# Loading Q and K in gathered halves of 64 partitions in a one-core Q·Kᵀ kernel

## The chip, the core and the metric

The kernel runs on one core of a Trainium2 chip. A core has a matrix engine (PE, with its weight loads shown as PEld), a vector engine (DVE), a scalar engine (ACT), a general engine (POOL, GpSimd), a queue engine (SP), and 16 DMA engines that move data between HBM and the on-chip memory SBUF (128 partitions). Matrix results land in PSUM. The metric is the device time of one execution in microseconds (us); the median over several runs is compared. Beside it stands one profiled execution, from which all durations are taken.

## What is computed

For 8 batches of 12 heads, each with 1024 rows of 64 float32 values in Q and in K, the kernel computes all products of rows of Q with rows of K:

```python
q: (8, 12, 1024, 64) float32        k: (8, 12, 1024, 64) float32
return np.einsum('bhid,bhjd->bhij', q, k).astype(np.float32)   # (8, 12, 1024, 1024)
```

The inputs are 50.3 MB, the output 402.7 MB. The 96 heads are written as 4 MB each.

## The kernel before

**Blocks and heads.** The 96 heads are worked in nine blocks of 2, 2, 4, 8, 16, 16, 16, 16 and 16 heads (`sizes`). While the heads of one block are computed, Q and K of the next are loaded, cast to float16 and transposed. Q and K of a block stand in turn in one of two pairs of tiles (`qk_sb`), so that PE can read one block while the next is built.

**One head** (`scores`, L265 on). PE computes a head in four steps of two row tiles: each step has two weight loads (L436) and four matmuls (L439) into one half of PSUM. ACT copies each step's 128x2048 result into an output buffer (L297). When all four copies are done, SP issues the 4 MB store (L310). There are three output buffers (`o_sb`); ACT's first copy of a head waits until the store that last used its buffer has landed.

**Inputs of a block of 16 heads.** Q is loaded by one 4 MB DMA into the single input tile `x_sb` (32 KB in each of 128 partitions, L171); K later goes into the same tile, so its load waits until Q's casts have read the tile. POOL casts to float16 into one of three `half` tiles (L220): a chunk takes four casts of 32 partitions each, and a block has eight chunks, named (x, part, c): x is Q or K, `part` says which partitions it reads (0: 0 to 31 and 64 to 95; 1: 32 to 63 and 96 to 127), c is the half of the row. DVE transposes each chunk into `qk_sb` in 32x32 squares (L239). PE's first matmul of a block waits for all its transposes (`self.ready`).

**Order.** The order on each queue is the order in which the Python code records the instructions. `side` holds what is recorded after a given step of a given head: the transposes of the next block at the heads listed in `TURNS`, and the loads at the places in `LOADS`, which for blocks 4 and on is `{1: 1, 7: 1}`: behind step 1 of heads 1 and 7. Both loads are issued from ACT's queue, so the DMA instruction stands behind that step's copy. `to_half` records casts as soon as a chunk's load has been recorded and a `half` tile is due to come free. An `Engine` counts its finished instructions in a semaphore; `settle` makes an engine wait for its own.

**The last head** (`scores_split`, L316 on) is stored in two parts. Its first part goes out by a DMA of POOL (L374) that scatters rows by a list of indices, `place`, eight of which lie out of bounds; those rows are stored by four small DMAs.

```python
at = LOADS.get(i, {1: 1, 7: 1})
if n in at:
    side[at[n]] = side.get(at[n], []) + [lambda: next_load(act)]
```

Of the kernel before, what the change touches and what calls it, by code (L numbers as in the profile page):

```python
# [63 lines left out]
def kernel(  # L64
# [14 lines left out]
    of = out.rearrange("b h i j -> (b h) i j")  # L79

    sizes = [2, 2, 4, 8] + [16] * ((BH - 16) // 16)
    PE_BLOCKS, EARLY = 2, 3
    NMAX = max(sizes)
    CHUNK, HALVES = 64 * 32, 3
    TURNS = (3, 4, 5, 6, 10, 11, 12, 13)
    APART = (16, 48)
    LOADS = {0: {}, 1: {}, 2: {1: 3}, 3: {2: 1}}

    pool = ctx.enter_context(tc.tile_pool(name="sb", bufs=1))
    psum = ctx.enter_context(  # L90
# [8 lines left out]
    ]  # L99
    o_sb = [pool.tile([P, NT, S], F32, name=f"o_sb{i}", tag=f"out{i}") for i in range(3)]  # L100
    rest_q = pool.tile([P, 64], F16, name="rest_q", tag="rest_q")
    place_sb = pool.tile([P, 1], I32, name="place", tag="place")
    place_f = pool.tile([P, 1], F32, name="place_f", tag="place_f")
    ps_all = psum.tile([P, 4 * S], F32, tag="po")
# [35 lines left out]
    input_busy = []  # L140
    outs = Ring(o_sb)
    input_landing = [Landing(nc, f"x{i}_in") for i in range(2)]
    tail_landing = Landing(nc, "tail_out")
    rest_landing = Landing(nc, "rest_out")
    store_landing = {id(t): Landing(nc, f"out{i}_out") for i, t in enumerate(o_sb)}

    class Block:
        def __init__(self, i, first, N):
            self.i, self.first, self.N = i, first, N
            self.by_pe = i < PE_BLOCKS  # L150
            self.R = N * S // P
            self.elems = self.R * D
            self.cut = max(1, -(-self.R * 32 // CHUNK))
            self.raw = [None] * 2
            self.landed = [[] for _ in range(2)]
            self.rows = [None] * 2
            self.halves = {}
            self.qk = qk_sb[i % 2]
            self.ready = []
            self.over = []  # L160

        def load(self, x, eng, landing=None):
            events = []
            if self.raw[x] is None:
                at = x * self.elems if self.i == EARLY else 0
                self.raw[x] = x_sb[:, at : at + self.elems]
                landing = input_landing[x]
                events = list(input_busy)
            src = flat[x][self.first * S : (self.first + self.N) * S]
            eng.wait(events)  # L170
            dma = eng.eng.dma_start(  # L171
                out=self.raw[x], in_=src.rearrange("(p r) d -> p (r d)", p=P)
            )
            self.landed[x].append(landing.start(dma))

        def load_head(self, n, x, eng, landing):
            start = (self.first + n) * S
            m = S * D // P
            dma = eng.eng.dma_start(
                out=self.raw[x][:, n * m : (n + 1) * m],  # L180
                in_=flat[x][start : start + S].rearrange("(p r) d -> p (r d)", p=P),
            )
            self.landed[x].append(landing.start(dma))

        def cast_rows(self, x):
            n = S * D // P
            buf, events, busy = rooms.next()
            rows = buf[:, : 2 * n].rearrange("p (r h d) -> p r h d", h=2, d=D)
            for h in range(2):
                done = gps.run(  # L190
                    lambda: nc.gpsimd.tensor_copy(  # L191
                        out=rows[:, :, h],
                        in_=self.raw[x][:, h * n : (h + 1) * n].rearrange(
                            "p (r d) -> p r d", d=D
                        ),
                    ),
                    events + [self.landed[x][h]],
                )
            self.rows[x] = rows, done, busy
            return done  # L200
# [9 lines left out]
        def cast_quads(self, x, part, c):  # L210
            m = self.R // self.cut
            buf, events, busy = (rooms if self.i == PE_BLOCKS else halves).next()
            dst = buf[:, : m * 32]
            raw = self.raw[x].rearrange("p (r h d) -> p r h d", h=2, d=32)
            for half in range(2):
                b = 2 * half + part
                for h in range(2):
                    q0 = 32 * (2 * half + h)
                    done = gps.run(
                        lambda: nc.gpsimd.tensor_copy(  # L220
                            out=dst[q0 : q0 + 32].rearrange("p (r d) -> p r d", d=32),
                            in_=raw[32 * b : 32 * b + 32, c * m : (c + 1) * m, h],
                        ),
                        events + self.landed[x],
                    )
            self.halves[x, part, c] = dst, done, busy
            if self.i >= EARLY:
                input_busy[:] = [done]
            return done
# [35 lines left out]
        def scores(self, n, side, regions, w):  # L265
            half, g = divmod(n, self.N // 2)
            cs = slice(half * D, (half + 1) * D)
            qT = self.qk[0].rearrange("c (g m t) -> c g t m", t=NT, m=P)
            kT = self.qk[1].rearrange("c (g j) -> c g j", j=S)
            buf, out_free, out_busy = outs.next()  # L270
            written = {}
            for u in range(NT // w):
                ps, ps_free, ps_busy = regions.next()
                for tt in range(w):
                    stationary = qT[cs, g, w * u + tt]
                    done = pe.run(
                        lambda: load_weights(stationary, half * D),
                        self.ready if n == 0 and u == 0 else [],
                        signal=False,
                    )  # L280
                    for j in range(2):
                        at = tt * S + j * 512
                        done = pe.run(
                            lambda: multiply(
                                ps[:, at : at + 512],
                                stationary,
                                kT[cs, g, j * 512 : (j + 1) * 512],
                                half * D,
                            ),
                            ps_free,  # L290
                            signal=tt == w - 1 and j == 1,
                        )
                dst = buf[:, w * u : w * u + w].rearrange("p t j -> p (t j)")
                by_dve = w == 1 and u % 2
                copier = dve if by_dve else act
                copied = copier.run(
                    lambda: (nc.vector.tensor_copy if by_dve else nc.scalar.copy)(  # L297
                        out=dst, in_=ps[:, : w * S]
                    ),
                    out_free + [done],  # L300
                )
                written[copier] = copied
                ps_busy.append(copied)
                for do in side.get(u, []):
                    do()
            self.over = [done]
            sp.wait(written.values())
            if self.first + n == 0:
                sp.wait(blocks[EARLY].landed[0])
            dma = nc.sync.dma_start(  # L310
                out=of[self.first + n].rearrange("(p t) j -> p (t j)", p=P),
                in_=buf.rearrange("p t j -> p (t j)"),
            )
            out_busy.append(store_landing[id(buf)].start(dma))
# [145 lines left out]
    for b in blocks[:EARLY]:  # L460
# [7 lines left out]
        else:  # L468
            for x in range(2):
                b.load(x, sp, Landing(nc, f"e{b.i}{x}"))  # L470
    stream = [(b, x) for b in blocks[EARLY:] for x in range(2)]

    casts = [
        (i, c) for i in range(PE_BLOCKS, len(blocks)) for c in blocks[i].chunks()
    ]

    def next_load(eng):
        if stream:
            b, x = stream.pop(0)
            earlier = (b.i, 0) if x else (b.i - 1, 1)  # L480
            assert b.i == EARLY or not any((i, c[0]) == earlier for i, c in casts)
            b.load(x, eng)

    for x in range(2):
        next_load(sp)
# [17 lines left out]
    def to_half(last):  # L503
        while casts:
            i, c = casts[0]
            if i > last or (blocks[i], c[0]) in stream:
                return
            if not (rooms if i == PE_BLOCKS else halves).free():
                return
# [9 lines left out]
    def block(i, heads, regions, w):  # L519
        b = blocks[i]  # L520
        nxt = blocks[i + 1] if i + 1 < len(blocks) else None
        for n in heads:
# [11 lines left out]
            elif nxt:  # L534
# [1 line left out]
                at = TURNS if i > EARLY else [m * b.N // len(parts) for m in range(len(parts))]  # L536
                some = [s for m, s in zip(at, parts) if m == n]
                side = {0: [lambda s=s: transposed(nxt, s) for s in some]}
            at = LOADS.get(i, {1: 1, 7: 1})
            if n in at:  # L540
                side[at[n]] = side.get(at[n], []) + [lambda: next_load(act)]
            if i == len(blocks) - 1 and n == b.N - 1:
# [5 lines left out]
    for b in blocks[:PE_BLOCKS]:  # L548
        for x in range(2):
            b.cast_rows(x)  # L550
    nc.gpsimd.wait_ge(gps.sem, gps.count)
    to_half(2)

    quarters = Ring([ps_all[:, i * S : (i + 1) * S] for i in range(4)])
# [6 lines left out]
    halves_ps = Ring([ps_all[:, 2 * S :], ps_all[:, : 2 * S]])  # L561
    halves_ps.busy = [quarters.busy[2] + quarters.busy[3], quarters.busy[0] + quarters.busy[1]]
    block(0, [1], halves_ps, 2)
    for i in range(1, len(blocks)):
        block(i, range(blocks[i].N), halves_ps, 2)
    sp.wait([(c, c.count) for c in [*store_landing.values(), tail_landing, rest_landing]])
# [30 lines left out]
```

## Time and profile before

| | |
|---|---|
| median of 3 runs | 1059.84 us (1059.79 to 1059.84) |
| the profiled execution's own time | 1060.67 us |
| its span, first to last instruction | 1058.9 us |
| PE, ACT, DVE, POOL busy | 66%, 66%, 41%, 34% of the span |
| moved between HBM and SBUF | 453.21 MB, mean 428 GB/s |
| chain that ended last | DMA 65%, ACT 15%, PE 8%, DVE 6%, POOL 4% |

All durations come from the profiled execution. In the profile a group of instructions is named by its line, engine, operation and tiles (written tile first); "idle before" is the time its engine stood still just before it, with what ended that. DMA queue q1 belongs to SP, q10 to ACT, q0 to POOL. The trace also holds a record of each DMA packet with queue, size, start and duration. It doesn't name the DMA engine, but packets of one engine follow each other so closely that they can be strung together by their ends and starts.

### The profile page before, as it was taken

How to read it: one execution, taken by the hardware profiler on the slowest of the kernel's cores; microseconds unless marked ns; L12 is line 12 of the kernel's file. 1: busy time of each engine (PE TensorE's matmuls, PEld its weight loads, DVE VectorE, ACT ScalarE, POOL GpSimd, SP SyncE). 2: the span in 40 equal slices, each digit the busy share in tenths (PEclk: the TensorE clock that was granted, in tenths of full speed). 3: DMA queues.
4: the chain of work that ended last, by engine and by line, in shares of the span. 5: the costliest groups of instructions: out<-in, count | busy, mean ns of one | idle time of the engine just before them, and what ended most of it. 6: DMA issues, size and time to landing. Idle time of an engine off the chain costs nothing.

```text
span 1058.9 us, 3350 instructions
## 1 busy us (share of the span) xinstructions
PE 702.3 (66%) x1572; PEld 127.4 (12%) x802; DVE 435.4 (41%) x57; ACT 695.6 (66%) x385; POOL 358.3 (34%) x223
## 2 busy tenths in 40 slices
PE   6875754857477747657765756775674777787771
PEld 1111100111011101101110111110110111111110
DVE  2995939029194008539002917600580930000001
ACT  4766755857477748567765856775674777777771
POOL 7926555056280019065005609100822900000000
DMA  9999999999999999999999999999999999999998
GB/s 378 434 424 433 435 431 434 420 423 428 434 431 433 436 417 435 432 433 433 435 418 436 436 427 430 433 436 429 430 428 428 436 434 434 432 429 433 434 431 366
DMA packets 17186, 453.21 MB, mean 428 GB/s; under 512 B 1929, under 2 KB 1929, under 8 KB 2953
## 3 DMA queue, kind: packets, MB, share of 16 engines
q1 hardware_dynamic: 15008, 408.03, 89.5%
q10 hardware_dynamic: 2016, 42.99, 9.8%
q0 software_dynamic: 144, 1.97, 0.4%
q8 instruction: 9, 0.15, 0.0%
q14 instruction: 9, 0.07, 0.0%
HBM read 50.33 MB, written 402.78 MB: 428 GB/s over the span
## 4 chain that ended last, share of the span: by engine, by line
DMA 65%; ACT 15%; PE 8%; DVE 6%; POOL 4%; issue 1%; SPq 0%; ACTq 0%
DMA out_dram<-o_sb 60%; ACT o_sb L297 15%; PE ps_all L439 7%; DVE kT L239 4%; POOL half L220 3%; DMA x_sb<-in_q_dram 2%; DMA x_sb<-in_k_dram 2%; DVE qT L239 1%; DMA o_sb<-in_q_dram 0%; DVE x_sb L345 0%; DVE o_sb L345 0%; PE ps_all L253 0%; POOL qT L191 0%; DVE kT L260 0%; ACT kT L260 0%
## 5 line engine op out<-in xcount | busy, mean ns | idle before, releaser
L439 PE MATMUL ps_all<-kT,qT 64*128 64x512 f16 x1536 | 696.4, 617 | 327.1 <-ACT o_sb L297 310.0
L297 ACT COPY o_sb<-ps_all 128x2048 f32<-128x2048 f32 (+1 forms) x380 | 687.7, 1859 | 331.6 <-DMA out_dram<-o_sb 286.3
L220 POOL CAST half<-x_sb 32x2048 f16<-32x2048 f32 x176 | 332.5, 1889 | 482.7 <-DMA x_sb<-in_q_dram 307.9
L239 DVE STREAM_TRANSPOSE qT<-half 128x2048 f16<-128x2048 f16 x22 | 202.5, 9477 | 274.0 <-POOL half L220 274.0
L239 DVE STREAM_TRANSPOSE kT<-half 128x2048 f16<-128x2048 f16 x22 | 202.4, 9536 | 132.6 <-POOL half L220 132.6
L436 PEld LDWEIGHTS <-qT 64*128 64x128 f16 x768 | 124.0, 162 | 896.3 <-issue 875.9
L345 DVE COPY x_sb<-ps_all 128x2048 f32<-128x2048 f32 x1 | 2.3, 2292 | 174.0 <-PE ps_all L439 174.0
L374 POOL DMA_INDIRECT out_dram<-x_sb,place x1 | 1.2, 1157 | 176.6 <-DVE x_sb L345 176.6
L239 DVE STREAM_TRANSPOSE kT<-kT 128x1024 f16<-128x1024 f16 x2 | 9.3, 4856 | 0.0
L239 DVE STREAM_TRANSPOSE qT<-qT 128x1024 f16<-128x1024 f16 x2 | 9.2, 4782 | 0.0
L220 POOL CAST qT<-o_sb 32x1024 f16<-32x1024 f32 x8 | 8.3, 1036 | 1.1 <-DMA o_sb<-in_q_dram 0.7
L220 POOL CAST kT<-o_sb 32x1024 f16<-32x1024 f32 x8 | 8.3, 1036 | 0.5
L260 DVE COPY qT<-ps_all 128x1024 f16<-128x1024 f16 x2 | 2.4, 1224 | 11.4 <-PE ps_all L253 11.4
L253 PE MATMUL ps_all<-ident,qT 128*128 128x128 f16 x16 | 2.1, 311 | 7.1 <-POOL qT L191 7.0
L297 DVE COPY o_sb<-ps_all 128x1024 f32<-128x1024 f32 x4 | 4.9, 1225 | 4.4 <-PE ps_all L439 4.4
L345 ACT COPY x_sb<-ps_all 128x2048 f32<-128x2048 f32 (+1 forms) x2 | 3.7, 1860 | 2.1 <-PE ps_all L439 2.1
L260 ACT COPY kT<-ps_all 128x1024 f16<-128x1024 f16 x1 | 1.0, 1013 | 5.1 <-PE ps_all L253 5.1
L366 POOL COPY rest_q<-qT 64x8 f16<-64x8 f16 x4 | 0.6, 197 | 9.9 <-DVE kT L239 9.9
L345 DVE COPY o_sb<-ps_all 128x2048 f32<-128x2048 f32 x1 | 2.3, 2292 | 3.7 <-PE ps_all L439 3.7
L191 POOL CAST qT<-o_sb 128x512 f16<-128x512 f32 x4 | 2.3, 614 | 4.0 <-DMA o_sb<-in_q_dram 4.0
L260 ACT ACT_TABLE_LOAD x1 | 1.3, 1283 | 2.8 <-issue 2.8
L260 DVE COPY kT<-ps_all 128x1024 f16<-128x1024 f16 x1 | 1.2, 1225 | 4.4 <-PE ps_all L253 4.4
(18 smaller groups left out, 14.5 us busy)
## 6 DMA issues: line engine op xcount, KB each, us to landing
out_dram<-o_sb SPq DMA_DIRECT2D x95, 4096.0 KB, 21.8
x_sb<-in_q_dram ACTq DMA_DIRECT2D x5, 4096.0 KB, 25.2
x_sb<-in_k_dram ACTq DMA_DIRECT2D x5, 4096.0 KB, 23.4
x_sb<-in_q_dram SPq DMA_DIRECT2D x1, 2048.0 KB, 14.5
x_sb<-in_k_dram SPq DMA_DIRECT2D x1, 2048.0 KB, 18.9
out_dram<-o_sb SPq DMA_DIRECT2D x1, 2048.0 KB, 17.4
o_sb<-in_k_dram ACTq DMA_DIRECT2D x4, 256.0 KB, 5.2
o_sb<-in_q_dram SPq DMA_DIRECT2D x4, 256.0 KB, 5.4
```

Of the source, the lines that this page charges most:

```text
L191: lambda: nc.gpsimd.tensor_copy(out=rows[:, :, h], in_=self.raw[x][:, h * n : (h + 1) * n].rearrange("p (r d) -> p r d", d=D),),
L220: lambda: nc.gpsimd.tensor_copy(out=dst[q0 : q0 + 32].rearrange("p (r d) -> p r d", d=32), in_=raw[32 * b : 32 * b + 32, c * m : (c + 1) * ...
L239: lambda: nc.vector.transpose(out=dst, in_=buf.rearrange("p (r i) -> p r i", i=32)),
L253: lambda: nc.tensor.transpose(t_ps[:, t], rows[:, t], ident),
L260: lambda: copy(out=dst, in_=t_ps.rearrange("c t m -> c m t")), [done]
L297: lambda: (nc.vector.tensor_copy if by_dve else nc.scalar.copy)(out=dst, in_=ps[:, : w * S]),
L345: lambda: (nc.vector.tensor_copy if copier is dve else nc.scalar.copy)(out=dst[:, t * S : (t + w) * S], in_=ps[:parts, : w * S]),
L366: lambda: nc.gpsimd.tensor_copy(out=packed[:, t, 0, :, c], in_=rows[:, t, :, c]),
L374: nc.gpsimd.indirect_dma_start(out=out.rearrange("b h (m t) j -> (b h m) (t j)", t=T), out_offset=bass.IndirectOffsetOnAxis(ap=place_sb, a ...
L436: return nc.tensor.ldweights(stationary, tile_position=(at, to))
L439: return nc.tensor.add_instruction(mybir.InstMatmult(name=nc.get_next_instruction_name(), ins=[nc.tensor.lower_ap(moving), nc.tensor.lower ...
```

## The change

Blocks 0 to 4 are loaded as before. From block 5 on, the load of Q or of K becomes two gathers of POOL's DMA queue, each over all 128 partitions of `x_sb`, with a list of 128 row indices in which the indices of 64 partitions lie out of bounds. The gather for part 0 has valid rows in partitions 0 to 31 and 64 to 95, the one for part 1 in the others, which are the partitions that the casts of that part read. The lists, two columns for each of the four blocks, are written once by POOL (an iota and four memsets). Each cast now waits for its own part's load.

The loads of blocks 4 to 7 for the block after them stand at step 2 of heads 0, 4, 8 and 11, and the transposes at heads 2, 3, 6, 7, 10, 11, 13 and 14. In POOL's queue a gather stands behind all casts recorded before it. It waits for ACT to have finished the copies recorded so far (the third copy of that head) and for POOL's own instructions. ACT issues only block 4's two loads. The instructions of PE, SP and DVE, and their order, stay as they were.

```diff
-    TURNS = (3, 4, 5, 6, 10, 11, 12, 13)
+    TURNS = (2, 3, 6, 7, 10, 11, 13, 14)
     LOADS = {0: {}, 1: {}, 2: {1: 3}, 3: {2: 1}}
+    LATER = {0: 2, 4: 2, 8: 2, 11: 2}
...
+        def load_part(self, x, part):
+            self.raw[x] = x_sb[:, : self.elems]
+            c = 2 * (self.i - WHOLE - 1) + part
+            gps.count += 1
+            dma = nc.gpsimd.indirect_dma_start(
+                out=self.raw[x],
+                out_offset=None,
+                in_=flat[x].rearrange("(p r) d -> p (r d)", r=self.R),
+                in_offset=bass.IndirectOffsetOnAxis(ap=rows_sb[:, c : c + 1], axis=0),
+                bounds_check=BH * S // self.R - 1,
+                oob_is_err=False,
+                engine_sem=gps.sem,
+            )
+            self.landed[x][part].append(part_landing[part].start(dma))
+            gps.settle()
...
-                        events + self.landed[x],
+                        events + self.landed[x][part],
...
     def next_load(eng):
-        if stream:
-            b, x = stream.pop(0)
+        if not stream:
+            return
+        b, x, part = stream.pop(0)
+        pending = [(i, c[0], c[1]) for i, c in casts if i >= EARLY]
+        if b.i <= WHOLE:
             earlier = (b.i, 0) if x else (b.i - 1, 1)
-            assert b.i == EARLY or not any((i, c[0]) == earlier for i, c in casts)
+            assert b.i == EARLY or earlier not in [c[:2] for c in pending]
             b.load(x, eng)
+        else:
+            assert pending[:1] in ([], [(b.i, x, part)])
+            gps.wait([(act, act.count)])
+            gps.settle()
+            b.load_part(x, part)
...
-            at = LOADS.get(i, {1: 1, 7: 1})
+            at = LOADS.get(i, LATER)
...
     block(0, [1], halves_ps, 2)
+    gps.settle()
+    gps.run(
+        lambda: nc.gpsimd.iota(
+            rows_sb,
+            pattern=[[P, G], [0, 2]],
+            base=blocks[WHOLE + 1].first * S // blocks[WHOLE + 1].R,
+            channel_multiplier=1,
+        )
+    )
+    gps.settle()
+    by_part = rows_sb.rearrange("p (g h) -> p g h", h=2)
+    for p in range(0, P, 32):
+        gps.run(
+            lambda: nc.gpsimd.memset(by_part[p : p + 32, :, 1 - p // 32 % 2], 2 * BH * S)
+        )
+    gps.settle()
```

More of the change, by code (lines that the diff above doesn't have):

```diff
@@ L81 @@
     sizes = [2, 2, 4, 8] + [16] * ((BH - 16) // 16)
-    PE_BLOCKS, EARLY = 2, 3
+    PE_BLOCKS, EARLY, WHOLE = 2, 3, 4
     NMAX = max(sizes)
     CHUNK, HALVES = 64 * 32, 3
-    TURNS = (3, 4, 5, 6, 10, 11, 12, 13)
+    TURNS = (2, 3, 6, 7, 10, 11, 13, 14)
     APART = (16, 48)
     LOADS = {0: {}, 1: {}, 2: {1: 3}, 3: {2: 1}}
+    LATER = {0: 2, 4: 2, 8: 2, 11: 2}
     pool = ctx.enter_context(tc.tile_pool(name="sb", bufs=1))
@@ L101 @@
     rest_q = pool.tile([P, 64], F16, name="rest_q", tag="rest_q")
+    G = (BH - sum(sizes[: WHOLE + 1])) // NMAX
+    rows_sb = pool.tile([P, 2 * G], I32, name="rows", tag="rows")
     place_sb = pool.tile([P, 1], I32, name="place", tag="place")
@@ L142 @@
     input_landing = [Landing(nc, f"x{i}_in") for i in range(2)]
+    part_landing = [Landing(nc, f"part{i}_in") for i in range(2)]
     tail_landing = Landing(nc, "tail_out")
@@ L154, in __init__ @@
             self.raw = [None] * 2
-            self.landed = [[] for _ in range(2)]
+            self.landed = [[[], []] for _ in range(2)]
             self.rows = [None] * 2
@@ L173, in load @@
             )
-            self.landed[x].append(landing.start(dma))
+            event = landing.start(dma)
+            for part in self.landed[x]:
+                part.append(event)
+        def load_part(self, x, part):
[13 more added lines that the diff above has]
+            gps.settle()
         def load_head(self, n, x, eng, landing):
@@ L182, in load_head @@
             )
-            self.landed[x].append(landing.start(dma))
+            self.landed[x][0].append(landing.start(dma))
         def cast_rows(self, x):
@@ L196, in cast_rows @@
                     ),
-                    events + [self.landed[x][h]],
+                    events + [self.landed[x][0][h]],
                 )
@@ L308, in scores @@
             if self.first + n == 0:
-                sp.wait(blocks[EARLY].landed[0])
+                sp.wait(blocks[EARLY].landed[0][0])
             dma = nc.sync.dma_start(
@@ L470 @@
                 b.load(x, sp, Landing(nc, f"e{b.i}{x}"))
-    stream = [(b, x) for b in blocks[EARLY:] for x in range(2)]
+    stream = [
+        (b, x, part)
+        for b in blocks[EARLY:]
+        for x in range(2)
+        for part in range(1 if b.i <= WHOLE else 2)
+    ]
     casts = [
@@ L505, in to_half @@
             i, c = casts[0]
-            if i > last or (blocks[i], c[0]) in stream:
+            if i > last or (blocks[i], c[0], c[1] * (i > WHOLE)) in stream:
                 return
@@ L550 @@
             b.cast_rows(x)
-    nc.gpsimd.wait_ge(gps.sem, gps.count)
+    gps.settle()
     to_half(2)
@@ L563 @@
     block(0, [1], halves_ps, 2)
+    gps.settle()
[13 more added lines that the diff above has]
+        )
+    gps.settle()
     for i in range(1, len(blocks)):
```

## Prediction

> **What bounds the kernel now.** I read the page's DMA rows first, then the stages, the waits and the chain. The share of the 16 DMA engines by slices, and the queues:
>
> ```profile
> DMA  9999999999999999999999999999999999999998
> ...
> q1 hardware_dynamic: 15008, 408.03, 89.5%
> q10 hardware_dynamic: 2016, 42.99, 9.8%
> q0 software_dynamic: 144, 1.97, 0.4%
> ```
>
> q1 holds what SP issues (the stores), q10 what ACT issues (the loads), q0 what POOL issues. The shares sum to 99.7%: nearly every DMA engine carries a packet at nearly every moment. The stages (busy us of PE, PEld, DVE, ACT, POOL, then clock, DMA share, GB/s) say the same; no compute engine fills its stage:
>
> ```profile
> 60.00:200.00 140.00, 86.50 (x192) 15.31 (x95) 96.80 (x11) 86.64 (x49) 64.21 (x34) 1.00 1.00 430
> 376.00:552.00 176.00, 116.14 (x258) 20.74 (x128) 73.57 (x8) 116.34 (x64) 60.46 (x32) 1.00 1.00 431
> 830.00:1030.00 200.00, 149.78 (x332) 26.64 (x166) 27.47 (x4) 149.81 (x84) 16.40 (x24) 1.00 1.00 432
> ```
>
> The waits agree. ACT, the only engine that feeds stores, waits for output buffers, so engines that seem late here are being held by the DMA:
>
> ```profile
> ACT o_sb L297 <- DMA out_dram<-o_sb: 286.3, 84, 8.9
> ```
>
> In the trace's packet records a 32 KB packet takes 1.213 us, and packets of one engine start 1.209 us apart with no gap. A completion packet (4 bytes) adds 6 ns. So the time is the DMA work of an engine, plus about 2 us before the first stores can run and about 2 us in which engines end unevenly (the first at 1053.8, the last at 1057.3). Only three things can move it: DMA work, its evenness over the engines, or an engine that finds no packet.
>
> **What the change does to the DMA work.** The bytes stay: blocks 5 to 8 had 8 loads of 128 rows of 32 KB, now 16 gathers with 64 valid rows each, 1024 packets both times (64 per engine). The trace has one such transfer, the scatter of the last head, whose list has 8 indices out of bounds (its group, then its row among the DMA issues with the us from issue to landing):
>
> ```profile
> L374 POOL DMA_INDIRECT out_dram<-x_sb,place x1 | 1.2, 1157 | 176.6 <-DVE x_sb L345 176.6
> ```
>
> ```profile
> out_dram<-x_sb,place POOLq DMA_INDIRECT x1, 18.6
> ```
>
> Its 144 packets on q0 are 120 of 16384 bytes (0.611 us) and 24 of 4 bytes (9 ns): 16 completions and 8 rows out of bounds. An index out of bounds thus costs a 4-byte packet. The 8 stood on one engine, each behind one store packet (1.22 us apart). Their partitions are 16-19 and 48-51, so rows p and p+32 share an engine, and a gather of partitions 0-31 and 64-95 should leave 4 valid rows on each of the 16: no engine gets more than another.
> - Added short packets per engine: 16 x (4 out of bounds + 1 completion) - 8 x 1 = 72, x 6 ns = **+0.4 us** (+0.65 at their full 9 ns). Were rows cut into 16 KB packets, 64 x (2 x 0.611 - 1.213) = +0.6 more; I take no cut, as the scatter's rows were not cut.
> - Slow reads. In the stretches of these 8 loads, packets exceeded 1.213 us by 2.95 us (loads) and 0.95 us (stores beside them), meaned over 16 engines: 3.36 us of it in the four Q loads, at heads 1 to 3 of a block, and 0.54 in the four K loads at heads 7 to 9. Nothing shows whether Q's data or the place in the block is the reason. If Q, nothing changes; if the place, the second half of Q escapes (-1.7) and the four places may all be quiet (-2.8) or all as bad (+2.8). I take **-0.7**, between no change and half of Q's excess. Bounds: -3.9 (all gone) and +2.8.
>
> **What it moves on the other engines.** ACT loses 8 issues of 0.33 us: ACT idles 2.3 us a head for its buffer, so 0. POOL gains 16 x 1.16 = 18.6 us of issue, one iota and four memsets. The issues fall where POOL waits for a load or for ACT's signal, and the casts behind them are counted below. The five setup instructions stand before the casts of block 3's last chunk, where POOL waits 3.79 us for DVE (52.3 to 56.1); at the last head the same kinds take 0.13 (iota) and 0.15 us (memset), about 1.1 us with the settling between them, so 0. Were that cover gone, block 4's Q load, issued at 63.83 right behind these casts, and with it block 4's start, which has no cover left (below), would come up to 1.1 us later, with up to 1.1 us on the end. SP's queue and PE's order stay; DVE's transposes keep their order, and DVE does nothing else there.
>
> The added waits: POOL waits for ACT's third copy of heads 0, 4, 8, 11, then issues. Behind it in POOL's queue stand only the casts of that quarter, behind these the transposes, behind them PE at the next block. Whether the DMA runs out of packets there is decided by the last two quarters, which come close together. The rows for casts and transposes are these (start, us):
>
> ```profile
> 459.30 31.13 POOL L220 CAST half<-x_sb 32x2048 f16<-32x2048 f32 x16 [35.77 <-DMA x_sb<-in_k_dram]
> ...
> 467.06 36.80 DVE L239 STREAM_TRANSPOSE kT<-half 128x2048 f16<-128x2048 f16 x4 [30.06 <-POOL half L220]
> ```
>
> that is 7.8 us for the 4 casts of a chunk, 15.6 a quarter, and 9.2 us a transpose. A gather's landing is an estimate: first packet 5.0 us after issue (scatter: 1034.74 to 1039.8), up to 1.2 for the store packet in front, 4 data rows each with a store packet (2.42 each), 4 short ones and the completion behind one store packet each (1.21): 5.0 + 1.2 + 9.7 + 6.1 = 22.0 us. From the third issue: landed 22.0; cast 37.6; ACT's signal for the fourth comes at 3 heads x 9.76 + 4.9 of load work = 34.2, so POOL is later and issues at 37.6; landed 59.6; first chunk cast 67.4; two transposes 85.8; PE's first four matmuls (1.9) 87.7. ACT's buffer for the next block is free 8 x 9.76 + 2 x 4.9 - 5.7 = 82.2 after the third issue. **The block starts 5.5 us late.** What that costs, block 4 shows today:
>
> ```profile
> 169.21 18.23 DVE kT L239 x2
> 187.44 0.05 issue
> 187.49 1.94 PE ps_all L439 x4
> ...
> 189.44 1.88 ACT o_sb L297
> ```
>
> The buffer's last store packet was done at 180.5, so ACT was 9.0 us late, and the store queue just covered it: the busy engines fell from 16 to 14 for one moment at 197.75. The cover is two stores of 9.7 us in the queue, less ACT's 7.5 and the issue. So 5.5 costs nothing; it costs from 9 us (fastest engines) to 11 us (the slowest, which sets the end).
>
> **Sum.** On the profiled execution: span 1058.9 + 0.4 - 0.7 = 1058.6. That execution took 1060.67 us, 0.83 over the median of the runs; I carry the difference over: 1059.84 - 0.3 = **1059.5 us**.
>
> [...]
>
> **Rivals.**
> - *Slower: the fourth quarter lands too late.* Place: the start of blocks 5 to 8. It decides when ACT is over 9 to 11 us late; two landings stand in series, so 2 to 3 us more per landing suffice. At 25.2 us (a whole load's median landing today) ACT is 11.9 late, which costs 0.9 to 2.9 at four starts: +4 to +12, say 1067.5. One reason would be a gather's issue held by a transpose that runs beside it: the third is issued 4.3 us before DVE is done with the second quarter, the fourth 1.4 or 10.6 us before the end of one or both transposes of the third, so 11.2 to 20.4 us late, +1 to +46, about 1083 in the middle. [...] Against: casts, which use SBUF too, take 1886 to 1895 ns whether a transpose runs beside them or not. Chance 0.23, of it 0.05 for the held issue.
> - *Faster: the slow reads go.* All 3.9 us gone, 0.4 added: 1056.3. For it: K's loads have almost none, so reads beside stores need not be slow. Against: half the loads still stand near the places that are slow now. Chance 0.20 for more than 2.1 us.
> - *It doesn't do what it says.* Rows out of bounds move data after all: 16 x 64 packets more, 64 x 1.21 = +77 us, 1137. Against it the 4-byte packets. Chance 0.01; 0.01 for gather rows that move slower than the scatter's.
> - *As forecast*, within 0.2% (2.1 us; about what a measurement of this kernel can tell from no change): 0.55.
>
> Range: 1056.3 (slow reads gone) to 1068 (late by a slower landing); outside lie about 0.1 above and 0.05 below. Faster 0.20, same 0.55, slower 0.25.
>
> **What would show it.** Right: q0 holds 16 x 144 + 144 = 2448 packets with 33.55 + 1.97 MB, DMA share 1.00 in every stage, ACT's wait for PE at block starts about 5 us and no slice below 410 GB/s after the first. Wrong: landings over 25 us, ACT's waits for PE over 9 us at blocks 5 to 8 and a DMA share under 1.00 just after them; or a higher q0 share than 64 x 1.213 us an engine gives (7.3% of the span, with the scatter 7.8%), which would mean slower reads.

## The result, and the profile after

The changed kernel takes **1067.62 us** (median of 6 runs, 1066.58 to 1073.12) against 1059.80 us for the kernel before in the same series (6 runs, 1059.56 to 1059.84): ratio 1.0083, 95% interval 1.0061 to 1.0105, **7.8 us slower**. The forecast was 1059.5; its range reached 1068.0. The profiled execution of the changed kernel took 1066.58 us, the fastest of its six runs, with a span of 1064.3 us; against the profiled execution before that is 5.91 us more.

The page of the changed kernel, the same rows as before: busy tenths and GB/s of the DMA in 40 slices, then the queues with packets, MB and share, then the HBM counter.

```profile
DMA  9999999999999999999999999999999999999997
GB/s 374 433 434 433 434 432 433 431 433 410 432 432 433 432 430 425 432 433 429 433 415 432 421 432 432 430 433 417 427 425 426 433 427 426 432 433 431 432 433 334
...
q1 hardware_dynamic: 15008, 408.03, 89.3%
q0 software_dynamic: 2448, 35.53, 8.2%
q10 hardware_dynamic: 864, 9.44, 2.1%
...
HBM read 83.89 MB, written 402.78 MB: 457 GB/s over the span
```

The packets on q0 are the 2448 that were forecast, with 33.55 + 1.97 MB: each index out of bounds cost a 4-byte packet here (9 ns) and moved nothing (453.21 MB before and after). Their share is 8.2% of the span, where the prediction named more than 7.8% as its sign of slower reads. (The HBM counter shows 83.89 MB read, before 50.33: it counted the 16 x 64 rows of 32 KB, 33.55 MB, that were never moved.) The shares still sum to 99.6%, but of a longer span: q0 and q10 now take 10.3% of 1064.3 us, before 10.2% of 1058.9. The stages (PE, PEld, DVE, ACT, POOL, clock, DMA share, GB/s) look almost as before:

```profile
60.00:200.00 140.00, 87.15 (x193) 15.36 (x95) 96.45 (x11) 87.27 (x49) 64.85 (x35) 1.00 1.00 431
376.00:552.00 176.00, 116.25 (x257) 20.74 (x128) 73.87 (x8) 116.42 (x65) 64.37 (x36) 1.00 1.01 430
830.00:1030.00 200.00, 145.29 (x322) 25.92 (x160) 36.88 (x4) 145.49 (x81) 31.60 (x32) 1.00 1.00 431
```

A full DMA share with 1 GB/s less: the engines carried a packet all the time but for 0.39 us between 190 and 1040 us, yet some packets took longer (3.25 us more in all; table below). A loss of 0.5% can hide in that. The waits (us in total, times, longest) show what is new on the other engines; the first row is the kernel before, the others the changed one:

```profile
ACT o_sb L297 <- PE ps_all L439: 41.4, 107, 11.4
...
ACT o_sb L319 <- DMA out_dram<-o_sb: 259.1, 75, 11.5
...
POOL x_sb L186 <- ACT o_sb L319: 114.7, 10, 22.1
ACT o_sb L319 <- PE ps_all L461: 71.8, 116, 10.3
```

ACT's waits for PE rose from 41.4 us to 71.8: blocks 5 to 8 start late. The start of block 8 in the timeline (start, us; the bracket is the idle time before):

```profile
873.80 18.42 DVE L261 STREAM_TRANSPOSE kT<-half 128x2048 f16<-128x2048 f16 x2 [19.95 <-POOL half L242]
...
892.28 3.63 PE L461 MATMUL ps_all<-kT,qT 64*128 64x512 f16 x8 [9.74 <-DVE kT L261]
...
894.24 3.63 ACT L319 COPY o_sb<-ps_all 128x2048 f32<-128x2048 f32 x2 [9.79 <-PE ps_all L461]
```

PE waits for the last two transposes, ACT for PE. ACT's longest waits for PE at the four starts were 6.3, 6.7, 8.1 and 9.8 us; less the 2.1 to 2.3 us that ACT waits for its buffer anyway, blocks 5 to 8 started 4.1, 4.5, 5.9 and 7.5 us late. The chain of waits of this page breaks off at the gather at 844 us (its shares sum to some 18%), so nothing is read from it.

**Where the 5.9 us are.** The packet records were strung into 16 engines as in the prediction. "Slow" is the time by which 32 KB packets after 190 us exceed 1.213 us, meaned over 16 engines, loads and stores apart; "idle" the time without a packet between 190 and 1040 us; "uneven" the last engine's end less the mean end; "end" from the last packet to the end of the span; "outside" the execution's own time less its span. All in us:

| kernel (profiled execution) | own time | slow loads | slow stores | short packets | idle | uneven | end | outside |
|---|---|---|---|---|---|---|---|---|
| before | 1060.67 | 2.95 | 1.54 | 0.72 | 0.06 | 1.87 | 1.62 | 1.78 |
| changed | 1066.58 | 4.45 | 3.29 | 1.16 | 0.39 | 2.33 | 2.84 | 2.23 |
| *again* | 1068.12 | 5.95 | 2.69 | 1.16 | 1.25 | 2.15 | 2.84 | 2.22 |
| *earlier* | 1065.90 | 3.17 | 3.28 | 1.16 | 0.19 | 3.17 | 2.85 | 2.23 |
| *earlier2* | 1063.96 | 2.52 | 3.73 | 1.16 | 0.11 | 1.52 | 2.84 | 2.23 |
| *pairs_early* | 1066.62 | 4.01 | 2.88 | 1.16 | 0.20 | 3.28 | 2.86 | 2.16 |
| *whole_pool* | 1063.38 | 3.57 | 1.50 | 0.72 | 0.12 | 3.63 | 2.19 | 1.79 |
| *late12* | 1080.65 | 8.50 | 2.25 | 1.16 | 12.18 | 1.36 | 2.85 | 2.23 |

Changed less before: 1.50 + 1.75 + 0.44 + 0.33 + 0.46 + 1.22 + 0.45 = 6.15, against 5.91 (the rest lies before 190 us, where 32 KB packets exceeded 1.213 us by 0.16 us and not by 0.87). So four things grew: slow loads, slow stores, the end (with what lies outside), and a little of everything else. The other rows are the experiments below.

### The profile page after: what moved, and what is told of

Same layout as the page of the kernel before. It is cut to its first block, busy times and chain, and to the rows that moved or that the text cites. A ratio compares the mean times of both kernels' runs of the same rounds, so it can differ in the third digit from the quotient of the medians.

```text
span 1064.3 us, 3404 instructions
## 1 busy us (share of the span) xinstructions
PE 702.4 (66%) x1572; PEld 127.5 (12%) x802; DVE 436.8 (41%) x57; ACT 695.6 (65%) x385; POOL 374.4 (35%) x244
## 2 busy tenths in 40 slices
DMA packets 18337, 453.21 MB, mean 426 GB/s; under 512 B 3080, under 2 KB 3080, under 8 KB 4104
## 3 DMA queue, kind: packets, MB, share of 16 engines
q0 software_dynamic: 2448, 35.53, 8.2%
HBM read 83.89 MB, written 402.78 MB: 457 GB/s over the span
## 5 line engine op out<-in xcount | busy, mean ns | idle before, releaser
L186 POOL DMA_INDIRECT x_sb<-in_q_dram,rows x8 | 8.3, 1032 | 88.8 <-ACT o_sb L319 86.0
L186 POOL DMA_INDIRECT x_sb<-in_k_dram,rows x8 | 8.0, 1006 | 32.1 <-ACT o_sb L319 28.7
```

Source lines behind the costliest of these rows:

```text
L186: dma = nc.gpsimd.indirect_dma_start(out=self.raw[x], out_offset=None, in_=flat[x].rearrange("(p r) d -> p (r d)", r=self.R), in_offset=ba ...
```

## The experiments

Three theories came out of the first two rows of this table. **LATE**: the late starts cost the time, by idle engines and a slow restart. **HALVES** (first held under the name SLOW, slow packets beside four loads a block): the halves make packets slow wherever they stand. **END**: DMAs issued by POOL cost a fixed time at the program's end. All ratios are to the kernel before, run beside each on the same chip; its medians there were 1060.0, 1060.2, 1060.2 and 1060.7 us.

**again**: the changed kernel unaltered.

> The changed kernel unaltered, to see a second execution in the trace and how far its times spread. Three theories of the 7.8 us. LATE: in most executions blocks 5 to 8 start later than the store queue covers; the profiled one (1066.6, the fastest of six) had lateness of 4.1 to 7.5 us and only 0.25 us of idle DMA. Then a slower execution shows block starts over 8 us late and DMA idle of a microsecond or more behind them. SLOW: packets are slower; then a slower execution shows the same block starts and more time over 1.213 us per packet (profiled: 9.5 us, meaned over the engines, against 6.7 before). END: POOL's drain at the end (1.46 us against 0.14) and what lies outside the span (2.3 against 1.8) are a fixed price of POOL's gathers, 1.8 us in every execution. Expected: median 1066 to 1069, and the split between LATE and SLOW read from this trace.

1067.09 us, ratio 1.0079 (1.0053 to 1.0106). ACT's waits at the starts of blocks 5 and 6:

```profile
ACT o_sb L319 <- PE ps_all L461: 9.8, 4, 9.3
ACT o_sb L319 <- PE ps_all L461: 10.3, 3, 9.9
```

These starts were 7.1 and 7.8 us late, and the engines idled 0.47 and 0.63 us behind them; blocks 7 and 8 were 6.1 and 5.6 us late, with 0.05 and none. The Q gathers that follow the two late starts had their first packet 1.8 to 2.0 us after issue (others 3.7 to 5.3) and were 1.0 to 1.1 us slow each, nearly all of it in the first row on each engine. Both LATE and slow packets are at work; END is the same to 0.01.

**earlier** and **earlier2** (one kernel, run twice): each load a head earlier.

```diff
-    TURNS = (2, 3, 6, 7, 10, 11, 13, 14)
+    TURNS = (2, 3, 5, 6, 9, 10, 12, 13)
-    LATER = {0: 2, 4: 2, 8: 2, 11: 2}
+    LATER = {0: 2, 3: 2, 7: 2, 10: 2}
```

> The second, third and fourth gather stand one head earlier (heads 0, 3, 7, 10 for 0, 4, 8, 11), so a block is ready about 9.8 us sooner and no block of 5 to 8 should start late. LATE: the spread goes and the median falls to about 1063 to 1066. SLOW and END: 1066 to 1068, no change, though no block starts late.

> The kernel with the loads at heads 0, 3, 7 and 10, unaltered, a second time. It had 6.5 us of slow packets after 190 us and 1065.25 us. 'Halves or four places bring slow packets, without a late start': again 6 us or more, 1064.5 to 1066. If that excess was chance: 4.5 to 5.5 us and about 1063.5.

1065.25 us, ratio 1.0045 (1.0028 to 1.0061); the second time 1067.16 us, 1.0064 (1.0048 to 1.0080), 1.2 us above what was expected of it. ACT's wait for PE at the start of block 8 is gone in both profiles (*earlier2*, 880 to 910 us):

```profile
ACT o_sb L319 <- PE ps_all L461: 0.7, 4, 0.2
```

(Block 5 alone still starts late, by 0.8 and 1.4 us.) The loads' own excess is then 3.17 and 2.52 us, about that before the change (2.95), but the stores' is 3.28 and 3.73. So a loss of 4.8 and 6.8 us (by the ratios) stays without the late starts. By the ratios (1.0083 and 1.0079 with them, 1.0045 and 1.0064 without) they cost 1.6 to 4 us, and that loosely, since the intervals of *earlier2* overlap those of both series of the changed kernel. Runs of 1073 us, one in each series of the changed kernel, don't occur among the ten of *earlier*.

**late12**: the fourth quarter a head later, a larger dose for LATE.

```diff
-    LATER = {0: 2, 4: 2, 8: 2, 11: 2}
+    LATER = {0: 2, 4: 2, 8: 2, 12: 2}
```

(With the last transposes at heads 14 and 15.)

> The changed kernel with the fourth gather at head 12 instead of 11, so that blocks 5 to 8 start about 6 us later still. It doses LATE. The prediction's rule says that lateness is free up to 9 us and costs from 9 to 11 us on; with 4 to 8 us in the two profiled executions of the changed kernel, 10 to 14 us here, so idle DMA of 1 to 4 us at each of four starts: 1071 to 1080. If late starts cost nothing, 1067 as before.

1080.89 us, ratio 1.0183 (1.0160 to 1.0206). The wait at block 5, then stretches from just before each late start (columns as in the stages):

```profile
ACT o_sb L319 <- PE ps_all L461: 13.4, 1, 13.4
```

```profile
360.00:390.00 30.00, 19.91 (x45) 3.69 (x23) 9.03 (x1) 18.17 (x10) 1.01 (x1) 1.00 0.82 333
538.00:566.00 28.00, 15.89 (x36) 3.03 (x19) 11.24 (x2) 14.20 (x8) 1.62 (x2) 1.00 0.91 371
716.00:745.00 29.00, 15.84 (x36) 2.97 (x19) 12.30 (x2) 15.33 (x9) 2.67 (x2) 1.00 0.95 388
```

Here the DMA share does fall. At 11 us of lateness the engines idled 5.2, 2.9, 1.9 and 2.1 us behind the four starts, and the loads' excess rose to 8.50 us. The mechanism is what the prediction's slower rival described; the changed kernel stands at its edge.

**whole_pool**: the loads of before (whole, at heads 1 and 7), but as 8 POOL gathers with 128 valid indices.

```diff
-    LATER = {0: 2, 4: 2, 8: 2, 11: 2}
+    LATER = {1: 1, 7: 1}
...
-        for part in range(1 if b.i <= WHOLE else 2)
+        for part in range(1)
```

> POOL issues 8 gathers of all 128 rows, none out of bounds, at the places of the kernel before (heads 1 and 7, step 1) with its transposes; nothing is loaded in halves. END alone: 1060.5 to 1061.7 (1059.8 plus the end's price, less if it goes with the number of gathers). SLOW, if it comes from gathers as such: slow packets as in the changed kernel, 1063 to 1066. LATE: no late starts here, so 1060 to 1062.

1062.49 us, ratio 1.0021 (1.0008 to 1.0033). The same bytes on q0 in 1296 packets:

```profile
q0 software_dynamic: 1296, 35.52, 8.1%
```

Slow loads and slow stores stay within the range of kernels with whole loads (loads 2.95 to 4.02, stores 1.35 to 1.56 in six of them), so gathers as such didn't slow packets (3.57 and 1.50 us here). But the 2.2 us of the ratio are more than was expected, and the end accounts for 0.57 of them; in this profile the ends are 1.76 us more uneven than before, which stays unexplained. What the end does cost can be read directly. In the trace's records of instructions POOL's last drain takes 0.138 us in the kernel before (one POOL DMA, the scatter), 0.802 us here (9) and 1.457 us in the changed kernel (17): 0.083 and 0.082 us for each further DMA of POOL. END holds: from the last packet to the span's end it is 1.62, 2.19 and 2.84 us, so 1.2 to 1.3 us of the change.

**oob_alone**: the kernel before with 16 gathers added whose indices are all out of bounds, at heads 0, 13, 14 and 15 of blocks 4 to 7, into a spare tile. They load nothing.

```diff
+            if 4 <= i < len(blocks) - 1 and n in (0, 13, 14, 15):
+                side[2] = side.get(2, []) + [gather_none]
```

> The kernel before with 16 gathers added on POOL that load nothing: all 128 indices are out of bounds, into a small spare tile, at times when POOL is idle (heads 0, 13, 14, 15 of blocks 4 to 7). Short packets: 16 x 9 per engine x 6 ns = 0.9 us. END: drain 1.4 to 1.5 us and about 0.45 outside the span, 1.8 in all. If out-of-bounds rows cost more than their short packets, for example by slowing the stores beside them, it shows here: over 1063. Otherwise 1059.8 + 0.9 + 1.8 = 1062.5, with a quiet mean of the packets.

1063.31 us, ratio 1.0035 (1.0024 to 1.0047). Queue and HBM counter:

```profile
q0 software_dynamic: 656, 1.98, 0.5%
...
HBM read 50.86 MB, written 402.78 MB: 427 GB/s over the span
```

The drain is 1.457 us again; slow stores stay at 1.56. Here an engine got two short packets a gather, in the changed kernel five; at that dose, and with no rows moving among them, they don't bring the slow stores. The counter rose by 0.53 MB, the 16 x 128 rows of 256 bytes that weren't moved. What lies outside the span stayed at 1.78 us, so the 0.45 us there belong to something else in the kernels with 16 loading gathers; that is open. So is what this kernel lost besides: 3.1 us at the median, of which the end is 1.6 and short packets 0.2.

**swapped, place28, place49**: the kernel before with K loaded ahead of Q; with the loads at heads 2 and 8; at heads 4 and 9.

```diff
-    stream = [(b, x) for b in blocks[EARLY:] for x in range(2)]
+    stream = [(b, x) for b in blocks[EARLY:] for x in ((1, 0) if b.i > 4 else (0, 1))]
```

```diff
-            at = LOADS.get(i, {1: 1, 7: 1})
+            at = LOADS.get(i, {2: 1, 8: 1})
```

(In *swapped* the order of the chunks is turned as well; in *place28* and *place49* the transposes move to later heads with the loads, and *place49* has `{4: 1, 9: 1}`.)

> The kernel before with K loaded, cast and transposed ahead of Q from block 5 on; all else the same. It tells whether the slow reads belong to Q's data or to the place in the block (the prediction left it open). Q's data: the slow packets move to heads 7 to 9 with Q. The place: K now has 0.4 to 0.9 us a load at heads 1 to 3 and Q little. The time stays within 1 us of 1059.8 either way.

> The kernel before with its whole loads one head later (heads 2 and 8). Slow reads went with the place when K and Q were swapped. If they go with the first heads of a block, the first load has fewer here: 1058 to 1060. If they go with the first of two loads wherever it stands: no change, 1059.5 to 1060.5.

> The kernel before with its whole loads at heads 4 and 9. If slow reads go with the first heads of a block, none are left: excess after 190 us falls from 4.5 to under 2.5 and the time to 1057 to 1058.5, below the kernel before. If they go with the first of two loads: no change.

1060.44, 1060.33 and 1060.84 us; ratios 0.9998 (0.9989 to 1.0008), 1.0002 (0.9993 to 1.0012) and 1.0008 (0.9998 to 1.0018). With K first, K's loads were slow (0.83, 0.76, 0.42, 0.70 us) and Q's were not (0.04 to 0.24), so Q's data is not the reason. But at heads 2 and 8 and at heads 4 and 9 the first load of a block was still slow (0.39 to 0.77, 0.26 to 0.78), and at heads 4 and 9 the second too (up to 0.96); in *whole_pool*, at the old places, one second load had 0.81. The slow reads follow neither the tensor nor a head, and no place here is free of them. Why they come stays open.

**halves_act**: the halves of the change, each as two plain ACT DMAs of 32 partitions in place of a gather.

```diff
+            for p in (32 * part, 64 + 32 * part):
+                event = part_landing[part].start(
+                    nc.scalar.dma_start(out=self.raw[x][p : p + 32], in_=src[p : p + 32])
+                )
```

> The same halves at the same four places and the same transposes, but each half is two plain DMAs of 32 partitions on ACT's queue; no gather and no index out of bounds. END: no price, 1.8 us less than the changed kernel. SLOW, if it comes from the places and the halves: slow packets as in the changed kernel, 1063 to 1066; if from the gathers, about 1060. LATE: landings without the 4 to 6 us that short packets cost, POOL not holding the fourth load, so starts on time: about 1060 to 1062.

1102.82 us, ratio 1.0400 (1.0382 to 1.0417): a miss of 37 us for every theory. The GB/s slices:

```profile
GB/s 380 436 431 433 427 435 431 383 394 428 387 402 432 393 424 387 433 395 388 432 380 429 397 407 410 384 435 383 418 388 391 415 390 430 434 435 427 435 434 329
...
q10 hardware_dynamic: 2400, 42.99, 12.6%
```

946 of the 1024 load packets took over 1.3 us; the mean was 1.81 us, against 1.21 to 1.25 us in ten of the 16 gathers of the changed kernel (at most 1.49). Each DMA's 32 rows were spread over all 16 engines (1536 packets on q10 for 32 DMAs, so 32 rows and 16 completions each). A gather gave each engine 4 rows, of its own partitions if the gathers go by the scatter, whose rows out of bounds, at partitions 16 to 19 and 48 to 51, stood on one engine. No run varied that alone, so why these packets were slow isn't shown.

**cols_act, cols_pool**: halves by columns, all 128 partitions by 16 KB, at the four places of *earlier*; by plain ACT DMAs, and by 16 gathers with no index out of bounds.

```diff
+            n = self.elems // 2
...
+                out=self.raw[x][:, part * n : (part + 1) * n],
...
-                        events + self.landed[x][part],
+                        events + self.landed[x][c],
```

> Halves without gathers: each half is one plain DMA on ACT's queue of all 128 partitions and half of each row (16 KB packets, eight per engine), at heads 0, 3, 7, 10, so that no block starts late; the chunks are cast in the order of these halves. No gather, no index out of bounds. If loading in halves at four places is what makes packets slow: 1062 to 1064. If it isn't: 1059.5 to 1061, the spread of the kernel before.

> The same column halves at the same places, but as 16 gathers of POOL of 128 rows of 16 KB, none out of bounds. Against the run with gathers one head earlier (1065.3) it takes away only the out-of-bounds rows and the split by partitions; against the plain column halves it adds only POOL's gathers. END goes with the number of gathers (drain 0.14 us with 1, 0.80 with 9, 1.46 with 17): +1.3 us on the plain column halves, and 0.45 outside the span if that goes with 17 gathers. So if nothing is wrong with gathers but END: 1061 to 1063. If gathers as such slow packets: 1064 to 1066. If the out-of-bounds rows or the split do: 1061 to 1063 again, 2 to 4 below 1065.3.

1067.12 us, ratio 1.0071 (1.0054 to 1.0088), and 1069.26 us, 1.0078 (1.0061 to 1.0095), both above every range expected. Neither has late starts, *cols_act* has no gather: half loads cost without POOL and without indices out of bounds. The cost takes another form, though. In *cols_act* 299 stores took over 1.3 us, most of them behind and ahead of a 16 KB packet, and in *cols_pool* one engine ended 8.2 us after the mean. Two kernels slow by other routes show little of the change's own.

**pairs, pairs_early, pairs_early2** (the last two one kernel): both halves at one place, the second after the first has landed; at heads 1 and 7, then at heads 0 and 6.

```diff
-    LATER = {0: 2, 4: 2, 8: 2, 11: 2}
+    LATER = {0: 1, 6: 1}
...
+            gps.wait(b.landed[x][0] if part else [])
```

> The same 16 gathers with their out-of-bounds rows, but at two places a block (heads 1 and 7): the second half follows when the first has landed, and the casts wait for both. Late starts are ruled out. If the four places make the extra slow packets: the packets' excess after 190 us falls from 6.5 (one head earlier) to about 5, and the time is 1059.8 + 0.4 short + 1.8 END + 0.5 = 1062.5 to 1063.5. If the halves or the out-of-bounds rows make them: 1064.5 to 1066, as with gathers one head earlier.

> The two halves of a tensor are gathered at one place: Q's behind step 1 of head 0, K's behind step 1 of head 6, the second half after the first has landed, casts after both. One head earlier than the kernel in which the halves went at heads 1 and 7, whose blocks 6 to 8 started 7 to 9 us late; so a start may be 0 to 2 us late, which no idle DMA should follow. Theory 'four places': with two places a block, as before the change, the excess of slow packets after 190 us falls to that of the kernels with whole loads (4.5 to 5.5 us), and the median is 1062 to 1063.5 (drain 1.3, short packets 0.4, rest 0 to 1). Rival 'halves': 64 valid rows at a time and the short packets bring slow packets wherever they stand; excess 6.5 to 8.6 and 1065 or more.

> A second look at the kernel with both halves at one place, for a second profile: the excess of slow packets should lie within 1 us of the first one's, or the comparison between four places and halves can't be made from single profiles.

*pairs* was said to rule late starts out. It didn't: two landings in series took 43 to 45 us, its blocks 5 to 8 started 9.6, 7.6, 8.4 and 8.7 us late, it took 1070.64 us (1.0102, 1.0085 to 1.0119) and told nothing apart. ACT's waits for PE at the start of its block 8:

```profile
ACT o_sb L321 <- PE ps_all L463: 11.5, 4, 11.0
```

*pairs_early* has no late start from block 5 on (ACT's waits for PE in it at 350 to 375 us):

```profile
ACT o_sb L321 <- PE ps_all L463: 0.5, 3, 0.2
```

It took 1066.71 us, 1.0062 (1.0047 to 1.0077), with 6.91 us of slow packets in one profile and 6.90 in the other. (In *pairs_early2* block 5 started 1.2 us late.) Two places or four: the same loss. HALVES holds against the four places, as it was expected to: 6.5 to 8.6 us of slow packets and 1065 or more. All these kernels have their rows out of bounds beside the valid ones, so they don't tell the halves from the rows out of bounds.

**What is slow about halves** came from sorting the slow stores of all profiles by the packet that follows on the same engine. On each engine the store packet directly ahead of the *first* row of a load ran longer, by 68 to 180 ns in the mean; one between two rows of the same load did not (1 to 6 ns in the kernels of this table). In a gathered half there is also a first row behind short packets.

| kernel | such starts seen | store ahead: mean excess, ns | sum over 16 engines, us |
|---|---|---|---|
| whole loads (before, *whole_pool*, *swapped*, *place28*, *place49*, *oob_alone*) | 126 to 133 | 81 to 104 | 0.66 to 0.86 |
| *earlier* | 251 | 150 | 2.35 |
| *earlier2* | 248 | 180 | 2.79 |
| *pairs_early*, *pairs_early2* | 236, 232 | 138, 170 | 2.03, 2.47 |
| changed | 221 | 132 | 1.83 |
| with more or longer late starts (*again*, *pairs*, *late12*) | 201, 224, 194 | 128, 166, 68 | 1.61, 2.33, 0.82 |

Eight loads on 16 engines give 128 starts, 16 gathers 256, and in the kernels with few or no late starts each cost more (138 to 180 ns against 81 to 104). The column kernels, which have no index out of bounds, show about as many (some 257 in *cols_act* at 70 ns, 232 in *cols_pool* at 135), so the pattern came without the short packets too; their stores between two packets of one load ran 40 ns long as well.

Behind a late start the load itself ran long, and most of that lay in the first row on each engine (some 0.9 of 1.65 us in the changed kernel, nearly all in *again*). The first gathers of blocks 5 to 7, which follow the late starts, exceed by 1.10, 1.00 and 1.00 us in *again* (7.1, 7.8 and 6.1 us late) and by 1.49, 1.30 and 1.40 in *late12* (about 11 us late), but by 0.12, 0.62 and 0.91 in the profile of the changed kernel (4.1, 4.5 and 5.9 us late). The whole loads at these places before had 0.72, 0.68 and 0.37. Both patterns were found in the records after the runs; what the hardware does there isn't shown.

## Why the prediction was wrong

The step that failed is the slow reads: "I take **-0.7**, between no change and half of Q's excess." Slow loads and slow stores together came to +3.25 us in the profiled execution, beyond the bound of +2.8. The prediction asked whether Q's data or the place decides. Neither does (*swapped*, *place28*, *place49*). The runs showed two other things in its place. Loading in halves, so starting twice as many stretches of load rows, goes with 1.3 to 2.2 us more of slow stores where no or hardly any start is late, at two places or four (*earlier*, *pairs_early*), and 1.75 in the changed kernel; in the records 1.0 to 2.0 us of it stand directly ahead of the first rows. And late starts go with slow first rows behind them, clearly at 6 us of lateness and more (loads 1.00 to 1.49 us slow in *again* and *late12*). In the profiled execution itself the loads' +1.50 is only in part that: some 0.9 us stands in first rows behind late starts, while the largest excess, 1.13 us, is in the second gather of block 4, which follows none. That part can't be told from chance, since kernels with whole loads alone range from 2.95 to 4.02.

The other steps, one by one:
- *Bytes and packets*: right. 2448 packets, 33.55 + 1.97 MB; short packets +0.44 us against +0.4.
- *A gather's landing, 22.0 us*: right. From issue to first cast it was 19.4 to 22.8 us. The rows among the DMA issues, with the median to landing:

```profile
x_sb<-in_q_dram,rows POOLq DMA_INDIRECT x8, 21.5
x_sb<-in_k_dram,rows POOLq DMA_INDIRECT x8, 21.0
```

- *5.5 us late*: right. 4.1 to 7.5 in one profile, 5.6 to 7.8 in the other.
- *"So 5.5 costs nothing; it costs from 9 us"*: wrong, by 1.6 to 4 us at the median. In most starts that were 7 us late or more engines idled (0.19 to 0.63 us at 7.1 to 7.8), and the estimate had no term for the slow loads behind a late start. *late12* shows the price beyond the cover, *earlier* that 4.8 to 6.8 us are lost without it.
- *The end*: missing. The sum had no term for the drain (+1.3 us) or for what lies outside the span (+0.45).
- *ACT, POOL and the setup at nothing*: right. Block 4 began at 188.4 us, before 189.4.
- *Carrying 0.83 us over to the median*: wrong by 1.9 us. The profiled execution before lay 0.83 us over the median, that of the changed kernel 1.04 under it; such an offset belongs to an execution, not to the kernel. It is why 5.9 us were found and 7.8 are to be explained. The profile of *again*, which lies near the median, has the same terms, with more slow loads and idle time.
- *The four places "all quiet" or "all as bad"*: the right question with, by the pattern above, the wrong unit: places in place of starts.

Of the rivals, "the fourth quarter lands too late" gave 1067.5, close to the result by luck: its 25 us landings and 11.9 us of lateness didn't come, and most of the loss has other reasons. The held issue, a guess that no row of the profile before shows, didn't come either: seven of the 16 gathers ran within a transpose and took 1.005 to 1.007 us, and their first packets came 4.9 to 5.4 us after issue, the others' 3.5 to 5.4. Their groups, with the mean ns of one:

```profile
L186 POOL DMA_INDIRECT x_sb<-in_q_dram,rows x8 | 8.3, 1032 | 88.8 <-ACT o_sb L319 86.0
L186 POOL DMA_INDIRECT x_sb<-in_k_dram,rows x8 | 8.0, 1006 | 32.1 <-ACT o_sb L319 28.7
```

Of the 7.8 us at the median, then: END 1.2 to 1.3, read from the drain in every profile; short packets 0.4, counted; halves 1 to 2 of slow stores, shown by *pairs_early* and *earlier*; late starts 1.6 to 4, loosely bounded by *earlier* and *again*. The 0.45 outside the span is measured and not explained. Uneven ends make 0.46 in this profile; they differ by some 2 us from profile to profile even with whole loads (1.35 to 3.63), so the account isn't closed to better than that.

## What to carry to other kernels

Where the DMA engines are full, price a change by the packets: not their bytes alone, but how many times a stream of loads begins among stores, since that is where packets ran long here (stores ahead of first rows: 1.83 us in the changed kernel, 0.66 to 0.86 with whole loads). A share of 1.00 showed only that engines carried something; the loss stood in packet durations (+3.25 us). Moving DMAs to POOL's queue had a price at the program's end (+1.22 us) that no stage shows, and slack that "just covers" a wait on a model should be counted as spent.

## What the runs showed of the hardware that was not expected

- POOL's last drain grew by 0.08 us with each DMA that POOL issued (0.138, 0.802 and 1.457 us at 1, 9 and 17).
- The HBM read counter counted rows that an index out of bounds kept from moving: +33.55 MB in the changed kernel with the same 453.21 MB moved. Small rows out of bounds (256 bytes, 8 to an engine) came as one 32-byte packet; 32 KB rows as 4 bytes each.
- Plain loads of 32 partitions, at equal bytes, took 1.81 us a packet in place of 1.21 and cost 43 us; the reason isn't shown.
- The store packet ahead of the first row of a load ran 0.07 to 0.18 us long in the mean, those between its rows 0.001 to 0.006 (0.04 in the column kernels).
